# Order edges for the down steps, the scores and a convolution's weight split, and six gate/up pairs in the wide form, in a decoder layer of one core

## The chip, the cores and the metric

The kernel runs on one core of one Trainium2 chip. The metric is the device time of one launch in microseconds (us). The time of a kernel is the median of its runs; beside it stands one profiled execution, whose trace is what the tables and rows below come from. In the trace PE is TensorE's matmuls, PEld its weight loads, DVE VectorE, ACT ScalarE, POOL GpSimd and SP SyncE (which issues the weight transfers).

## The reference

One layer on `x` of 512 tokens by 1024 features, all in float32: a SwiGLU feed-forward, a merge of two token mixers (dilated attention and a gated linear recurrence), and a second feed-forward, with a norm before and after each.

```python
D_MODEL = 1024; SEQ = 512; N_ATTN_HEADS = 12; HEAD_DIM = 128; LRU_WIDTH = D_MODEL; CONV_WIDTH = 4; D_FF = 2816

def swiglu(x, w_gate, w_up, w_down):
    return (jax.nn.silu(x @ w_gate) * (x @ w_up)) @ w_down
...
    f = swiglu(rms_norm(h, ffn1_norm_pre[l]), ffn1_w_gate[l], ffn1_w_up[l], ffn1_w_down[l])
    h = h + 0.5 * rms_norm(f, ffn1_norm_post[l])
    u = rms_norm(h, mix_norm_pre[l])
    q, k, v, xr, yr, gl = jnp.split(u @ w_in[l], splits, axis=-1)
    ...  # attention in three groups of four heads (dilations 1, 4, 16), merged over the groups by their log-sum-exp
    attn_d = attn.astype(x.dtype).reshape(B, S, ATTN_OUT_WIDTH) @ w_attn_branch[l]
    rec = rg_lru_branch(xr, ...) * jax.nn.gelu(yr)       # convolution of width 4, two gates, a scan over the tokens
    rec_d = rec @ w_rec_branch[l]
    gates = jax.nn.sigmoid(gl).reshape(B, S, N_BRANCHES, D_MODEL)
    h = h + rms_norm((gates[:, :, 0] * attn_d + gates[:, :, 1] * rec_d) @ w_out[l], mix_norm_post[l])
    f = swiglu(rms_norm(h, ffn2_norm_pre[l]), ffn2_w_gate[l], ffn2_w_up[l], ffn2_w_down[l])
    return h + 0.5 * rms_norm(f, ffn2_norm_post[l])
```

## The kernel before

**Numbers.** Each float32 operand is split into a high part (its rounding to the fp32r type, written by an ACT copy, L302) and a low part (the rest, a DVE subtraction, L303). That pair of instructions is called a split. A product is then three matmuls into one PSUM tile: high by high, high by low, low by high (L729, L730, L731).

**Pairs.** Activations lie transposed, features on partitions and 512 tokens along the row. The 2816 hidden columns are 22 tiles, numbered f. For most f the gate tile and the up tile form a 2 by 2 block matrix (two halves of the inner dimension by gate and up), and the activations another (two halves of the inner dimension by two halves of the tokens, `HB` = 256). Their product is formed from seven products p1 to p7 in place of eight, each of four inner steps of 128 (`seventh`). The sums of weight blocks that this needs are made for each pair by `w_forms` on DVE (L691 to L696), followed by four splits called a, b, c, d: a is used by p1 and p2, b by p6 and p5, c by p7 and p4, d by p3. The raw weights of a pair are two transfers of 512 KB through SP into a ring of four `raw` tiles.

There are three ways to run a pair. `seven` keeps partial sums on DVE. `seven_on`, called narrow here, has its products in the order p1, p5, p6, p2, p7, p3, p4; it carries the sum on in PSUM: ACT copies a partial sum into the start of the next accumulator (L743), so that the following product adds to it. It is 84 matmuls of 256 columns. `seven_wide`, called wide here, takes the high and the low part of the activations in one matmul of 512 columns (L779) and the low weights by high activations in one of 256 (L780), with the two partial results in the two halves of a PSUM tile. It is 28 matmuls of each width; its partial sums are moved on as tiles of 512 columns (ACT, L784), and each result is folded from the two halves (ACT copy L790 and DVE addition L792; DVE L800 and the line after the branch in `sum_of`). It uses all five `acc` tiles of PSUM, `seven_on` four. The mixers' pairs (q and k, the two gates, the gated branch) are wide already. In the feed-forwards f = 0 to 5 (first) and 0 to 2 (second) are plain, f = 3 and 4 of the second are `seven`, and the rest are narrow.

**Down.** The down projection also runs by seven products, in four parts of four tiles f each (`SEVEN`, `STEPS_AT`), the last six tiles plainly. Each part has four steps i = 0 to 3; the step's weights are prepared by `d_forms` ("prepd") and used by `down7`, which issues 12 matmuls of 512 columns for each of its products (L1043 to L1045), 24 in most steps. The results are added up through `aux` tiles of PSUM: ACT copies a running sum into the tile before ("seeds", L1032) and out of it after (L1048). `ffn_order` writes out the order of the events: for each f the forms of the step, the forms of the next pair ("prep"), the pair ("prod"), the step.

**Order.** A scheduler fixes the order of the instructions on each engine when the kernel is built, by priorities. `tc.high_priority(offset=...)` raises what is inside: `AHEAD` = 100 for weight forms, `EVAC` = 200 for what empties PSUM. `tc.issue_after(ins)` keeps an instruction behind `ins` where both are on the same engine; it adds no semaphore. The order may therefore put a few matmuls of a down step, or of the scores of the attention (L1378 and L1379: first of head 0, ahead of a softmax), between two products of a pair. `state` is a dictionary in which the last split's instructions are kept under "split" (ACT) and "low" (DVE).

The convolution (`conv`) fetches the weights of each 128 columns with `fetch`, which splits them; the third group's first fetch stands beside the pair of the fourth gated branch, which is not wide.

Of the kernel before, what the change touches and what calls it, by code (L numbers as in the profile page):

```python
# [16 lines left out]
P = 128  # L17
# [3 lines left out]
NF = 22  # L21
FF_PARTS = ((0, 4), (4, 8), (8, 12), (12, 16), (16, 22))
NSTD = {1: 6, 2: 3}

SEVEN = range(4)
STEPS_AT = {1: ((6, 7, 7, 8), range(9, 13), range(13, 17), range(17, 21)),
# [4 lines left out]
HB = 256  # L31
# [152 lines left out]
def hybrid_layer(ctx: ExitStack, tc: tile.TileContext, xT: bass.AP, xN: bass.AP, wst: bass.AP,  # L184
# [537 lines left out]
    def seventh(t, w, p, ps, start):  # L722
        at = t[p].at
        if len(at(0, 0).shape) == 3:
            ps = ps.rearrange("q (b t) -> q b t", b=2)
        for k in range(4):
            ks = slice(k * P, (k + 1) * P)
            wh, wl, xh, xl = w[p][:, 0, ks], w[p][:, 1, ks], at(0, k), at(1, k)
            PE.matmul(ps, wh, xh, start=start and k == 0, stop=False, skip_group_check=True)  # L729
            PE.matmul(ps, wh, xl, start=False, stop=False, skip_group_check=True)  # L730
            PE.matmul(ps, wl, xh, start=False, stop=k == 3, skip_group_check=True)  # L731

    def seven_on(t, w, g0, g1, u0, u1):

        b, z, y, v = (acc_ps()[:, :HB] for _ in range(4))

        def copy(ps, dst=None):
            if dst is None:  # L740
                dst = tpool.tile([P, HB], F32, name="c", tag="c", bufs=CB)
            with tc.high_priority(offset=EVAC):
                ACT.activation(dst, ps, AF.Copy)  # L743
            return dst

        seventh(t, w, "p1", b, True)
        copy(b, y)
        seventh(t, w, "p5", z, True)
        c5 = copy(z)
        seventh(t, w, "p6", b, False)  # L750
        c6 = copy(b)
        seventh(t, w, "p2", y, False)
        g0(y)
        seventh(t, w, "p7", b, False)
        copy(b, v)
        u1(b, c5)
        seventh(t, w, "p3", z, False)
        g1(z, c6)
        seventh(t, w, "p4", v, False)
        u0(v)  # L760

    def seven_wide(t, w, g, u, seen=lambda ap: ap, then=lambda: None, sign=1.0):


        b, z, y, v, o = (acc_ps() for _ in range(5))

        def two(ps):
            return ps[:, :HB], ps[:, HB:]

        def product(p, ps, start):  # L770
            at = t[p].at
            part, cross = ps.rearrange("q (s c) -> q s c", s=2), two(ps)[1]
            if len(at(0, 0).shape) == 3:
                part = ps.rearrange("q (s b t) -> q s b t", s=2, b=2)
                cross = cross.rearrange("q (b t) -> q b t", b=2)
            for k in range(4):
                ks = slice(k * P, (k + 1) * P)
                wh, wl = w[p][:, 0, ks], w[p][:, 1, ks]
                PE.matmul(part, wh, at(BOTH, k), start=start and k == 0, stop=False, skip_group_check=True)  # L779
                PE.matmul(cross, wl, at(0, k), start=False, stop=k == 3, skip_group_check=True)  # L780

        def move(dst, src):
            with tc.high_priority(offset=EVAC):
                return ACT.activation(dst, src, AF.Copy).ins  # L784

        def fold(ps, dst=None, sign=1.0):
            out = tpool.tile([P, HB], F32, name="c", tag="c", bufs=CB) if dst is None else dst
            x, y_ = two(ps) if dst is None else map(seen, two(ps))
            with tc.high_priority(offset=EVAC):
                ACT.activation(out, x, AF.Copy, scale=sign)  # L790
                if sign > 0:
                    DVE.tensor_add(out, y_, out)  # L792
                else:
                    DVE.scalar_tensor_tensor(out, y_, sign, out, op0=ALU.mult, op1=ALU.add)
            return out

        def sum_of(dst, ps, c, sign=1.0):
            x, y_ = two(ps)
            with tc.high_priority(offset=EVAC):
                DVE.tensor_add(c, x, c)  # L800
                if sign > 0:
                    DVE.tensor_add(dst, seen(y_), seen(c))
                else:
                    DVE.scalar_tensor_tensor(dst, y_, sign, c, op0=ALU.mult, op1=ALU.subtract)

        product("p1", b, True)
        move(y, b)
        product("p5", z, True)
        c5 = fold(z)
        product("p6", y, False)  # L810
        move(v, y)
        c6 = fold(y)
# [46 lines left out]
    def ffn(n, x, r, forms_x, apool, pss):  # L859
# [82 lines left out]

        def prod(f, w):
            g, u = tmp("g"), tmp("u")
            if f >= FIRST_ON[n]:
                lo, hi = HALVES

                def g1(z, c6):
                    with tc.high_priority(offset=EVAC):
                        DVE.tensor_add(g[:, hi], z, c6)  # L950
                    ACT.activation(g[:, hi], g[:, hi], AF.Silu)

                def u1(b, c5):
                    with tc.high_priority(offset=EVAC):
                        DVE.tensor_add(u[:, hi], b, c5)

                def u0(v):
                    def put(dst, view):
                        for q, (h, src) in enumerate(zip(HALVES, (v, u[:, hi]))):
                            DVE.scalar_tensor_tensor(dst[:, q] if len(dst.shape) == 3 else dst[:, h], g[:, h], -1.0,  # L960
                                                     src, op0=ALU.mult, op1=ALU.mult)
                    into(f, put)

                seven_on(t, w, lambda y: ACT.activation(g[:, lo], y, AF.Silu), g1, u0, u1)
                return
            seven(t, w, acc_ps()[:, :HB], [g[:, h] for h in HALVES], [u[:, h] for h in HALVES])
            ACT.activation(g, g, AF.Silu)
            into(f, lambda dst, v: DVE.scalar_tensor_tensor(dst, v(g), -1.0, v(u), op0=ALU.mult, op1=ALU.mult))

# [64 lines left out]
        def down7(a, i, w):  # L1034
            x = sevens[a]
            gs = groups(i)
            for m, (p, k) in enumerate(gs):
                ps = seeded.pop((p, k))
                first = not follows(a, p)
                for j in range(2):  # L1040
                    xh, xl = (x[p][:, s_, j * HB + k * P:j * HB + k * P + P] for s_ in range(2))
                    wh, wl = (w[p][:, s_, j * T:(j + 1) * T] for s_ in range(2))
                    PE.matmul(ps, xh, wh, start=first and j == 0, stop=False, skip_group_check=True)  # L1043
                    PE.matmul(ps, xh, wl, start=False, stop=False, skip_group_check=True)  # L1044
                    PE.matmul(ps, xl, wh, start=False, stop=j == 1, skip_group_check=True)  # L1045
# [20 lines left out]

        keys = [(w, n, i) for i in range(NSTD[n]) for w in ("gate", "up")]
        forms = {}
        for ev in ffn_order(n):
            if ev[0] == "std":  # L1070
                j = ev[1]
# [6 lines left out]
                for step in steps[j:] if j == min(NSTD[n], 4) - 1 else steps[j:j + 1]:  # L1078
                    step()
            elif ev[0] == "prep":  # L1080
                forms[ev[1]] = w_forms(("gu", n, ev[1]))
            elif ev[0] == "prepd":
                forms[ev[1:]] = d_forms(*ev[1:])
            elif ev[0] == "seeds":
                for g in groups(ev[2])[:3]:
                    seed(ev[1], *g)
            elif ev[0] == "down7":
                down7(*ev[1:], forms.pop(ev[1:]))
            else:
                prod(ev[1], forms.pop(ev[1]))  # L1090
# [112 lines left out]
    with ExitStack() as mx:  # L1203
# [164 lines left out]
        def attend(hd, heads):  # L1368
# [6 lines left out]

            p0 = [facc[:, 0, :], facc[:, 1, :]]
            sp = [aux_ps(), aux_ps()]
            PE.matmul(sp[0][:, 0:128], q[0][:, 0:P], k[0][:, 0:P], start=True, stop=True)  # L1378
            PE.matmul(sp[0][:, 128:384], q[0][:, P:2 * P], k[0][:, 0:2 * P], start=True, stop=True)  # L1379
            for b in (2, 3):  # L1380
                PE.matmul(sp[1][:, (b - 2) * 256:(b - 1) * 256], q[0][:, b * P:(b + 1) * P],
# [127 lines left out]
    with ExitStack() as mx:  # L1509
# [44 lines left out]
        def conv(hd, then):  # L1554

            for c in (2 * hd, 2 * hd + 1):
                ps, w = acc_ps(), fetch(("in", 36 + c))
                if c % 2:
                    then()
                gemm(ps, w, um)  # L1560
# [300 lines left out]
```

## Time and profile before

| | us |
|---|---|
| median of 3 runs | 1209.59 |
| lowest to highest run | 1208.93 to 1209.86 |
| the profiled execution | 1209.61 |
| its span in the trace | 1207.8 |
| PE busy | 1198.6 (99%) |
| DVE busy | 1033.3 (86%) |
| ACT busy | 831.8 (69%) |
| weight transfers (512 KB), issue to landing | 3.5 |

The span is the stretch from the first to the last instruction in the trace; the execution is 1.81 longer than it. Busy time is the sum over an engine's instructions. The ends of matmuls are modelled, so neighbouring matmuls overlap in the rows: a matmul of 256 columns is shown as 0.28 long, and the next one starts 0.12 after it. Distances between starts are therefore what counts for PE. The mean granted clock of TensorE is 0.999 of full speed.

### The profile page before, as it was taken

The numbers are of one execution on the slowest core, as the hardware profiler recorded it, in microseconds if no ns is written. First come the engines' busy times: TensorE is split into PE (matmuls) and PEld (weight loads), VectorE is DVE, ScalarE is ACT, GpSimd is POOL, SyncE is SP. The second block draws the span as 40 slices with busy tenths as digits, with TensorE's granted clock in tenths as the row PEclk, the third lists the DMA queues.
The fourth block names the chain that finished last, engine by engine and source line by source line (L and its number), as shares of the span: only waits on it lengthen the run. The fifth ranks groups of instructions, "written<-read, shape, count | busy, mean of one in ns | idle before, by whom it ended". The sixth has DMA issues, their size and how long they took to land.

```text
span 1207.8 us, 18850 instructions
## 1 busy us (share of the span) xinstructions
PE 1198.6 (99%) x7222; PEld 1070.1 (89%) x7222; DVE 1033.3 (86%) x1626; ACT 831.8 (69%) x1447; POOL 26.1 (2%) x51
## 2 busy tenths in 40 slices
PE   9999999999999999999999999999999999999997
PEld 8889999999888888888888888888899999999996
DVE  7999888989689899999868999774799888889964
ACT  6566787887566576777736988734566687778763
POOL 0000000000011000000000000000100000000000
PEclk9999999999999999999999999999999999999999
DMA  7224343434725232222323532235443333333441
GB/s 267 88 92 139 120 139 109 137 117 150 250 106 154 71 101 91 89 87 80 122 67 110 176 121 88 88 107 189 140 142 121 121 125 117 128 120 126 125 173 70
DMA packets 45819, 149.77 MB, mean 124 GB/s; under 512 B 5152, under 2 KB 8608, under 8 KB 45728
## 3 DMA queue, kind: packets, MB, share of 16 engines
q1 hardware_dynamic: 38160, 131.09, 32.9%
q0 software_dynamic: 7280, 17.30, 4.3%
q8 instruction: 56, 0.92, 0.3%
q14 instruction: 35, 0.29, 0.1%
q10 hardware_dynamic: 288, 0.17, 0.0%
HBM read 138.06 MB, written 6.29 MB: 120 GB/s over the span
## 4 chain that ended last, share of the span: by engine, by line
PE 92%; DVE 4%; DMA 2%; ACT 1%; issue 1%; DVEq 0%; ACTq 0%
PE acc L779 10%; PE acc L729 9%; PE acc L731 9%; PE acc L730 9%; PE acc L315 7%; PE acc L317 7%; PE acc L316 7%; PE acc L780 5%; PE aux L1043 4%; PE aux L1044 4%; PE aux L1045 4%; PE acc L433 2%; PE acc L432 2%; PE acc L431 2%; DVE w L303 2%; DMA raw<-in_w 2%
## 5 line engine op out<-in xcount | busy, mean ns | idle before, releaser
L303 DVE TENSOR_TENSOR w<-raw,w 128x1024 fp32r<-128x1024 f32 (+1 forms) x272 | 296.9, 1097 | 32.2 <-ACT w L302 31.4
L302 ACT ACTIVATE w<-raw 128x1024 fp32r<-128x1024 f32 (+1 forms) x272 | 259.5, 958 | 90.0 <-PE acc L317 48.2
L729 PE MATMUL acc<-big,w 128*128 128x256 f32 x860 | 243.6, 283 | 0.0
L731 PE MATMUL acc<-big,w 128*128 128x256 f32 x860 | 243.4, 283 | 0.0
L730 PE MATMUL acc<-big,w 128*128 128x256 f32 x860 | 243.3, 283 | 0.0
L729 PEld LDWEIGHTS acc<-big,w 128*128 128x128 f32 x860 | 164.8, 192 | 1.8
L730 PEld LDWEIGHTS acc<-big,w 128*128 128x128 f32 x860 | 164.8, 192 | 1.5
L731 PEld LDWEIGHTS acc<-big,w 128*128 128x128 f32 x860 | 164.8, 192 | 0.0
L779 PE MATMUL acc<-big,w 128*128 128x512 f32 x380 | 136.5, 398 | 0.0
L780 PE MATMUL acc<-big,w 128*128 128x256 f32 x380 | 107.5, 283 | 0.0
L1043 PE MATMUL aux<-w,xf 128*128 128x512 f32 x224 | 87.3, 392 | 0.6 <-ACT w L302 0.6
L1044 PE MATMUL aux<-w,xf 128*128 128x512 f32 x224 | 87.5, 391 | 0.0
L1045 PE MATMUL aux<-w,xf 128*128 128x512 f32 x224 | 87.2, 389 | 0.0
L779 PEld LDWEIGHTS acc<-big,w 128*128 128x128 f32 x380 | 71.4, 188 | 16.0 <-ACT acc L784 0.2
L780 PEld LDWEIGHTS acc<-big,w 128*128 128x128 f32 x380 | 71.7, 189 | 0.3
L303 DVE TENSOR_TENSOR w<-s,w 128x1024 fp32r<-128x1024 f32 x51 | 62.2, 1220 | 3.2 <-ACT w L302 2.7
L315 PE MATMUL acc<-xf,w 128*128 128x512 f32 (+1 forms) x168 | 59.2, 354 | 0.0
L316 PE MATMUL acc<-xf,w 128*128 128x512 f32 (+1 forms) x168 | 58.7, 350 | 0.0
L317 PE MATMUL acc<-xf,w 128*128 128x512 f32 (+1 forms) x168 | 58.5, 349 | 0.0
L302 ACT ACTIVATE w<-s 128x1024 fp32r<-128x1024 f32 x51 | 53.9, 1057 | 6.2 <-PE acc L731 3.0
L779 PE MATMUL acc<-rb,w 128*128 128x512 f32 x152 | 55.5, 397 | 0.0
L743 ACT ACTIVATE c<-acc 128x256 f32<-128x256 f32 x68 | 25.8, 383 | 35.3 <-PE acc L731 35.3
(458 smaller groups left out, 2919.5 us busy)
## 6 DMA issues: line engine op xcount, KB each, us to landing
raw<-in_w SPq DMA_DIRECT2D x232, 512.0 KB, 3.5
big<-xf POOLq DMA_DIRECT2D x6, 512.0 KB, 3.3
gains<-in_rows POOLq DMA_DIRECT2D x5, 512.0 KB, 5.4
h<-in_x SPq DMA_DIRECT2D x8, 256.0 KB, 5.1
h<-in_xn POOLq DMA_DIRECT2D x4, 512.0 KB, 6.7
kept_m<-h POOLq DMA_DIRECT2D x4, 512.0 KB, 2.9
vals<-in_w SPq DMA_DIRECT2D x4, 512.0 KB, 6.0
h<-kept_m POOLq DMA_DIRECT2D x4, 512.0 KB, 6.2
```

What stands on the lines that cost most here:

```text
L302: state["split"] = ACT.activation(dh, src, AF.Copy).ins
L303: state["low"] = DVE.tensor_sub(dl, src, dh.bitcast(F32)).ins
L315: PE.matmul(ps, wh, xh, start=first, stop=False)
L316: PE.matmul(ps, wh, xl, start=False, stop=False)
L317: PE.matmul(ps, wl, xh, start=False, stop=last)
L729: PE.matmul(ps, wh, xh, start=start and k == 0, stop=False, skip_group_check=True)
L730: PE.matmul(ps, wh, xl, start=False, stop=False, skip_group_check=True)
L731: PE.matmul(ps, wl, xh, start=False, stop=k == 3, skip_group_check=True)
L779: PE.matmul(part, wh, at(BOTH, k), start=start and k == 0, stop=False, skip_group_check=True)
L780: PE.matmul(cross, wl, at(0, k), start=False, stop=k == 3, skip_group_check=True)
L1043: PE.matmul(ps, xh, wh, start=first and j == 0, stop=False, skip_group_check=True)
L1044: PE.matmul(ps, xh, wl, start=False, stop=False, skip_group_check=True)
```

## The change

It has four parts.

- Six pairs of the feed-forwards run as `seven_wide`: f = 10, 14, 18 in the first and 9, 13, 17 in the second, one in each cycle of four tiles, at the step i = 1 of a down part. Behind them stand one ACT silu and one DVE product of 512 columns in place of two of 256 each.
- Each matmul of `down7` is kept behind `state["product"]`, the last matmul of the last product written before it (p4 of the pair in front). In the same way the first scores' matmul of each head is kept behind the last product written before it.
- The weight forms of the next pair are kept behind the splits of the down step's weights ("prepd"), on ACT and on DVE.
- The fetch of the convolution's column block 4 is kept behind `state["kept"]`, the ACT copy of b into v of the last narrow pair (that of the fourth gated branch).

```diff
+WIDE = {1: (10, 14, 18), 2: (9, 13, 17)}
...
-            PE.matmul(ps, wl, xh, start=False, stop=k == 3, skip_group_check=True)
+            state["product"] = PE.matmul(ps, wl, xh, start=False, stop=k == 3, skip_group_check=True).ins
...
-                ACT.activation(dst, ps, AF.Copy)
+                state["copied"] = ACT.activation(dst, ps, AF.Copy).ins
...
         copy(b, v)
+        state["kept"] = state["copied"]
...
+                last = PE.matmul(cross, wl, at(0, k), start=False, stop=k == 3, skip_group_check=True)
+            state["product"] = last.ins
...
-            if f >= FIRST_ON[n]:
+            if f in WIDE[n]:
+                seven_wide(t, w, *([x[:, h] for h in HALVES] for x in (g, u)))
+            elif f >= FIRST_ON[n]:
...
+                    with tc.issue_after(state["product"]):
+                        PE.matmul(ps, xh, wh, start=first and j == 0, stop=False, skip_group_check=True)
+                        PE.matmul(ps, xh, wl, start=False, stop=False, skip_group_check=True)
+                        PE.matmul(ps, xl, wh, start=False, stop=j == 1, skip_group_check=True)
...
+        behind = []
...
-                forms[ev[1]] = w_forms(("gu", n, ev[1]))
+                with ExitStack() as edges:
+                    while behind:
+                        edges.enter_context(tc.issue_after(behind.pop()))
+                    forms[ev[1]] = w_forms(("gu", n, ev[1]))
             elif ev[0] == "prepd":
                 forms[ev[1:]] = d_forms(*ev[1:])
+                if True:
+                    behind[:] = [state["split"], state["low"]]
...
-            PE.matmul(sp[0][:, 0:128], q[0][:, 0:P], k[0][:, 0:P], start=True, stop=True)
+            with tc.issue_after(state["product"]):
+                PE.matmul(sp[0][:, 0:128], q[0][:, 0:P], k[0][:, 0:P], start=True, stop=True)
...
-                ps, w = acc_ps(), fetch(("in", 36 + c))
+                ps = acc_ps()
+                with tc.issue_after(state.pop("kept")) if hd == 2 and c == 4 else nullcontext():
+                    w = fetch(("in", 36 + c))
```

More of the change, by code (lines that the diff above doesn't have):

```diff
@@ L779, in product @@
                 PE.matmul(part, wh, at(BOTH, k), start=start and k == 0, stop=False, skip_group_check=True)
-                PE.matmul(cross, wl, at(0, k), start=False, stop=k == 3, skip_group_check=True)
+                last = PE.matmul(cross, wl, at(0, k), start=False, stop=k == 3, skip_group_check=True)
+            state["product"] = last.ins
         def move(dst, src):
@@ L965, in prod @@
                 return
-            seven(t, w, acc_ps()[:, :HB], [g[:, h] for h in HALVES], [u[:, h] for h in HALVES])
+            else:
+                seven(t, w, acc_ps()[:, :HB], [g[:, h] for h in HALVES], [u[:, h] for h in HALVES])
             ACT.activation(g, g, AF.Silu)
@@ L1042, in down7 @@
                     wh, wl = (w[p][:, s_, j * T:(j + 1) * T] for s_ in range(2))
-                    PE.matmul(ps, xh, wh, start=first and j == 0, stop=False, skip_group_check=True)
-                    PE.matmul(ps, xh, wl, start=False, stop=False, skip_group_check=True)
-                    PE.matmul(ps, xl, wh, start=False, stop=j == 1, skip_group_check=True)
+                    with tc.issue_after(state["product"]):
+                        PE.matmul(ps, xh, wh, start=first and j == 0, stop=False, skip_group_check=True)
+                        PE.matmul(ps, xh, wl, start=False, stop=False, skip_group_check=True)
+                        PE.matmul(ps, xl, wh, start=False, stop=j == 1, skip_group_check=True)
                 dst, sign = sum_at(p)
```

## The prediction

> **What bounds the kernel now.** I read the page first, then the waits of TensorE, then windows and timelines around each edit. Times are us. Section 1 and the engine line of section 4 (the chain that ended last):
>
> ```profile
> span 1207.8 us, 18850 instructions
> PE 1198.6 (99%) x7222; PEld 1070.1 (89%) x7222; DVE 1033.3 (86%) x1626; ACT 831.8 (69%) x1447; POOL 26.1 (2%) x51
> PE 92%; DVE 4%; DMA 2%; ACT 1%; issue 1%; DVEq 0%; ACTq 0%
> raw<-in_w SPq DMA_DIRECT2D x232, 512.0 KB, 3.5
> ```
>
> The reader sees that PE works nearly all the span and carries 92% of the chain. So only two things can shorten it: fewer or cheaper PE issues, and the few places where PE stands. DVE at 86% is the next bound; ACT and DMA have room. The last line (512 KB of weights, issue to landing) is needed further down. The waits of PE, the rows that answer to the edits (us in all, times, longest):
>
> ```profile
> PE aux L1378 <- DVE qk L792: 0.7, 1, 0.7
> PE aux L1043 <- ACT w L302: 0.6, 3, 0.2
> PE acc L729 <- ACT acc L743: 0.4, 1, 0.4
> ```
>
> These are exactly a scores' matmul, three down matmuls and a product waiting for a copy. A row counts only idle time behind the modelled end of the matmul before, so the real loss is larger; I take it from starts.
>
> The profiled run took 1209.61: the span of 1207.8 and 1.81 outside it. The median of the three runs is 1209.59, 0.02 away, so what is taken off the profiled run is taken off the median. 0.2% is 2.4: faster means under 1207.2, slower over 1212.0.
>
> **Part 1, six pairs in the wide form.** Windows: start:end, length, then busy time and instructions of PE, PEld, DVE, ACT, POOL, then granted clock, DMA share and GB/s. First a narrow pair, then two wide pairs of the gated branch that the kernel already has, then two cycles of four pairs with their down steps, one of each feed-forward.
>
> ```profile
> 181.05:191.12 10.07, 10.07 (x85) 10.07 (x84) 9.20 (x14) 7.88 (x15) 0.00 (x0) 1.00 0.32 106
> 623.18:642.78 19.60, 19.60 (x114) 17.06 (x112) 15.26 (x27) 15.43 (x24) 0.00 (x0) 1.00 0.28 88
> 224.95:284.39 59.44, 59.44 (x421) 56.07 (x420) 53.71 (x69) 47.53 (x82) 0.00 (x0) 1.00 0.36 121
> 1012.59:1072.68 60.09, 59.88 (x422) 56.19 (x421) 50.97 (x69) 46.66 (x81) 0.00 (x0) 1.00 0.37 122
> ```
>
> A narrow pair is 84 matmuls of 256 columns in 10.07, 0.120 each. A wide pair is 28 of 512 and 28 of 256 columns: 19.60 / 2 = 9.80. Six pairs save 6 x 0.27 = 1.6. The granted clock is 1.00 in all rows, so no clock differs between the forms.
>
> The Trainium skill has a rule that speaks against this size ("TensorE: Matmul & The Clock Gate", section "Wait — 56ns, not 53.3ns?"): warm back-to-back matmuls start N columns over 2.4 GHz plus about 2.5 ns apart, so joining two matmuls spares only the fixed part. As an estimate from that page, 28 fewer matmuls would save 28 x 2.5 ns = 0.07 a pair, 0.4 in all; the trace's 0.120 for 256 columns is more than that rule gives, so here the trace disagrees and decides.
>
> What the wide form adds lies on DVE and ACT. Groups by line (busy, mean ns, idle before and what ended it); the three of `seven_on` and the 128x512 one are from the window 165.51 to 224.95:
>
> ```profile
> L792 DVE TENSOR_TENSOR c<-acc,c 128x256 f32<-128x256 f32 x38 | 15.8, 419 | 5.3 <-ACT c L790 5.0
> L800 DVE TENSOR_TENSOR c<-acc,c 128x256 f32<-128x256 f32 x38 | 14.9, 416 | 0.6
> L955 DVE TENSOR_TENSOR u<-acc,c 128x256 f32<-128x256 f32 x4 | 1.7, 417 | 0.0
> L950 DVE TENSOR_TENSOR g<-acc,c 128x256 f32<-128x256 f32 x4 | 1.7, 416 | 0.0
> L960 DVE SCALAR_TENSOR_TENSOR tt<-g,acc 128x256 f32<-128x256 f32 x4 | 1.7, 414 | 0.0
> L925 DVE SCALAR_TENSOR_TENSOR tt<-tt 128x512 f32<-128x512 f32 x1 | 0.7, 684 | 0.0
> L784 ACT ACTIVATE acc<-acc 128x512 f32<-128x512 f32 x57 | 33.5, 588 | 14.2 <-PE acc L780 11.3 <-DVE e L1443 1.1 <-DVE xch L1421 1.1
> ```
>
> Narrow, DVE: u1, g1 and two products, 0.417 + 0.416 + 2 x 0.414 = 1.66. Wide: four folds (L792), two sums of two steps (L800), one product of 512 columns: 4 x 0.419 + 4 x 0.416 + 0.684 = 4.02. That is 2.36 more a pair. ACT has three moves of 0.588 (1.76) more; its four copies of 256 columns stay. The busiest cycle goes from 53.71 to 56.07 of DVE in about 59.2, 95%, the other quoted one to 53.3 in 59.8, 89%. DVE is therefore still not the bound of a cycle. On average the cost is nothing, hidden by 3.1 of free DVE time a cycle; the order of steps has to be looked at.
>
> That order I followed by hand behind a wide pair of the first feed-forward, whose last fold stands ahead of the next pair's weight forms on DVE. Let E be the end of its last product. The rows for the steps and, in the present order, how the same chain ends on ACT and what it is for on PE:
>
> ```profile
> L303 DVE TENSOR_TENSOR w<-raw,w 128x1024 fp32r<-128x1024 f32 x13 | 15.9, 1221 | 1.9 <-ACT w L302 1.9
> L692 DVE TENSOR_TENSOR s<-s,raw 128x512 f32<-128x512 f32 x4 | 2.8, 689 | 1.7 <-DMA raw<-in_w 1.7
> 216.92 1.05 ACT L302 ACTIVATE w<-raw 128x1024 fp32r<-128x1024 f32 x1
> 219.52 0.37 ACT L743 ACTIVATE acc<-acc 128x256 f32<-128x256 f32 x1
> 220.76 0.28 PE L729 MATMUL acc<-big,w 128*128 128x256 f32 x1
> ```
>
> Fold about 0.6, four weight sums of 0.69, a stt of 0.684 and two splits of 1.22 end at about E + 6.4. PE first does a down step of 24 matmuls at 0.228 (5.5) and p1 (1.44), and wants the b forms at E + 6.9: 0.5 left. The c split ends 1.22 later, E + 7.6, and lets the next gate weights start; they land 3.5 later, E + 11.1. Then on ACT come the a and b splits, a silu half and the copy of b into v. In the rows this stretch lasts from 216.92 to 219.89, 2.97; it would end near E + 14.1. PE wants that copy before p4, at E + 5.5 + 6 x 1.44 = E + 14.1 (in the rows the copy has 0.9 in hand). So this copy is due about when it is wanted. Between nothing (the splits run closer than in those rows) and 0.6 (landing a little late), three times; I take 0.1 to 0.15 each, near the lower end, since the sum closes to 0.0. Behind wide pairs of the second feed-forward the same sum leaves over 1.5, and it costs nothing.
>
> **Part 2, down behind the pair's product.** PE's timeline (start, length): a stand in the second feed-forward and, for the pace, an undisturbed down step; then pieces of the chain: the split in front of the stand, and the two other stands.
>
> ```profile
> 941.02 0.28 PE L731 MATMUL acc<-big,w 128*128 128x256 f32 x1
> 941.51 0.72 PE L1043 MATMUL aux<-w,xf 128*128 128x512 f32 x2 [0.21 <-ACT w L302]
> 942.07 0.28 PE L729 MATMUL acc<-big,w 128*128 128x256 f32 x1
> 147.22 0.40 PE L1043 MATMUL aux<-w,xf 128*128 128x512 f32 x1
> 147.46 0.40 PE L1044 MATMUL aux<-w,xf 128*128 128x512 f32 x1
> 940.51 0.95 ACT w L302
> 1014.39 0.73 PE aux L1043 x2
> 1074.48 0.73 PE aux L1043 x2
> ```
>
> Two down matmuls stand between p1 and p5 and want a split that ACT ends at 941.46. PE could have gone on at 941.14: 0.37 lost. The two then take 0.56 in place of 2 x 0.23, 0.10 more. So 0.47, three times by the waits (941.5, 1014.4, 1074.5): 1.4. Behind the pair's last product the split is over 8 old. What is late next? The copies of down's sums, and through them the seeds of the following groups; down steps already run so in most cycles, without a row in the waits. Nothing taken for it. The weight forms that the change puts behind a down split on ACT and DVE wait for what stood beside them: at most 0.3 at the first such pair (f6, product p7, behind two 128x1024 splits), taken as 0.1.
>
> **Part 3, scores behind a product.**
>
> ```profile
> 418.52 0.28 PE L780 MATMUL acc<-big,w 128*128 128x256 f32 x1
> 419.46 0.49 PE L1378 MATMUL aux<-qk 128*128 128x128 f32 x2 [0.66 <-DVE qk L792]
> 429.64 0.59 PE L1379 MATMUL aux<-qk 128*128 128x256 f32 x2
> 429.89 0.58 PE L779 MATMUL acc<-big,w 128*128 128x512 f32 x1
> 430.30 0.28 PE L780 MATMUL acc<-big,w 128*128 128x256 f32 x1
> ```
>
> The first scores could start at 418.64 and wait for the fold that writes q and k until 419.46: 0.82. The later pair of scores breaks a product: 429.89 to 430.30 is 0.41 where 0.23 is usual, 0.18. Behind the third pair's last product q and k are long folded. The softmax of head 0 starts later by about a pair; it has the next pairs to hide in. One break stays, 0.1. Gain 0.9; bounds 0.6 (the softmax pushes back 0.3) and 1.0.
>
> **Part 4, a convolution's weight split behind the copy.**
>
> ```profile
> 688.56 0.28 PE L731 MATMUL acc<-big,w 128*128 128x256 f32 x1
> 689.22 0.39 PE L729 MATMUL acc<-rb,w 128*128 128x256 f32 x1 [0.38 <-ACT acc L743]
> 687.84 1.05 ACT L302 ACTIVATE w<-raw 128x1024 fp32r<-128x1024 f32 x1
> 688.79 0.37 ACT L743 ACTIVATE acc<-acc 128x256 f32<-128x256 f32 x1
> ```
>
> p4 starts 0.54 late (688.68 to 689.22) because the copy stands behind a split of 1.05. With the copy ahead it ends about 688.7 and p4 stands for 0.1 at most: gain 0.43 (0.3 to 0.54). The split comes 0.4 later; its weights are next on PE after the rest of this pair, some microseconds on.
>
> **Sum.** 1.6 + 1.4 + 0.9 + 0.4 = 4.3, less 3 x 0.13 + 0.1 = 0.5: 3.8 to 3.9. 1209.6 - 3.9 = **1205.7**. Own range: all bounds good, 1.6 + 1.4 + 1.0 + 0.54 = 4.5, 1205.0; all bounds bad, 1.6 + 1.4 + 0.6 + 0.3 - 3 x 0.6 - 0.3 = 1.8, 1207.8.
>
> **The rivals.**
> - A: the joining of matmuls spares little among down steps, because the 0.27 was measured in an undisturbed stretch. Its bounds are 0 and 0.27 a pair; at the lower quarter, 0.07, 1.2 are missing: 1206.9. Against: both rows are dense. The skill's 2.5 ns, above, would come to the same place.
> - B: the copy behind wide pairs stalls at its upper bound, 3 x 0.6 = 1.8 where 0.4 is in the sum: 1207.1 to 1207.8. For: the sum closes to 0.0.
> - C: the edges only shift the stands to another product or down group (gain 0 from parts 2 to 4): 1209.6 - 1.6 + 0.5 = 1208.5. Against: every freed instruction is one whose data come early, by microseconds.
> - D, slower: DVE becomes the bound around the wide pairs. From the point where its lag behind E passes the 0.5 in hand at the b forms, each further microsecond stands on PE. If all of the 2.36 less 0.5 does so six times, 6 x 1.86 = 11.2 against 4.3: 1216.5. Against: 3.1 free a cycle, and the second feed-forward's larger room.
> - E: the build's order leaves something unmoved. The instruction order of the changed kernel shows six wide pairs and each moved step, so it is left at nearly nothing.
>
> **How the numbers follow.** Forecast 0.60, A 0.12, B 0.11, C 0.08, D 0.08, E 0.01. Faster: forecast 0.58, A 0.11, half of B 0.06, C 0.01: 0.76. Slower: D and a little more, 0.09. Within: 0.15. The range takes the forecast's good end with something for stands not counted (1204.0) and reaches past B and C's middle (1208.6); D and half of C stay out.
>
> **What would show it.** After: PE's waits without the L1378, L1043 and L729 rows above; six windows of about 9.80 in place of 10.07; about 7222 - 168 = 7054 matmuls; DVE busy up by 6 x 2.36 = 14 and ACT by about 10. Wrong would be: new waits of PE for DVE's splits (w L303) or for the copy into v right behind the wide pairs (B, D), wide windows above 10 (A, D), or waits of the same size at other products (C).

## The result, and the profile after

The changed kernel takes 1213.38 us (median of 8 runs, 1212.5 to 1214.18), the kernel before 1209.72 in the same runs: ratio 1.0029, 95% interval 1.002 to 1.0038. It is slower by 3.7 us; forecast was a gain of 3.9, to 1205.7, with a range of 1204.0 to 1208.6. The profiled execution took 1213.6, its span is 1211.8. Lines of the page after:

```profile
span 1211.8 us, 18611 instructions
PE 1200.5 (99%) x7054; PEld 1061.2 (88%) x7054; DVE 1044.6 (86%) x1656; ACT 840.0 (69%) x1459; POOL 26.1 (2%) x51
PE 86%; DVE 5%; ACT 5%; DMA 2%; issue 1%; DVEq 0%; ACTq 0%
raw<-in_w SPq DMA_DIRECT2D x232, 512.0 KB, 3.7
```

PE issues 168 matmuls fewer, as it should, and the span is 4.0 longer. DVE is busy for 11.3 more and ACT for 8.2 more, where 14 and about 10 were forecast. In the chain that ended last, ACT has gone from 1% to 5% and PE from 92% to 86%. The waits of PE after:

```profile
PE acc L730 <- ACT acc L744: 1.3, 2, 0.9
PE acc L730 <- ACT c L744: 1.2, 2, 0.6
PE aux L1418 <- DVE facc L1399: 0.3, 1, 0.3
PE acc L732 <- DVE w L304: 0.2, 1, 0.2
PE acc L781 <- DVE qk L805: 0.2, 1, 0.2
```

(Lines moved: L744 is L743 of before, L730 to L732 are L729 to L731, L304 is L303; L1418 is a later group of the scores.) The three rows that the edges were aimed at are gone, but for a rest at the convolution. New ones stand in their place: two waits for the copy of b into v (`acc`), two for the copy that p7 waits for (`c`). Where they lie is read from windows by stage (start:end, length, busy time and instructions of PE, PEld, DVE, ACT, POOL). The stages are the first feed-forward from its first pair, the attention from its first q and k pair, the pair beside the convolution, and the second feed-forward. First before, then after, then three pairs after: f = 11, f = 12 and the wide f = 14.

```profile
72.26:310.00 237.74, 237.74 (x1681) 224.29 (x1680) 210.27 (x277) 182.50 (x309) 3.28 (x6) 1.00 0.41 133
407.36:601.19 193.83, 193.17 (x1189) 171.05 (x1188) 181.86 (x403) 137.91 (x305) 0.00 (x0) 1.00 0.30 96
680.00:690.74 10.74, 10.36 (x86) 10.14 (x84) 10.74 (x17) 9.98 (x16) 2.16 (x4) 1.00 0.61 213
898.55:1168.69 270.14, 269.52 (x1934) 255.04 (x1933) 235.56 (x314) 200.28 (x340) 2.66 (x5) 1.00 0.40 130
```

```profile
72.10:314.12 242.02, 239.31 (x1598) 220.18 (x1597) 216.16 (x293) 186.15 (x315) 3.28 (x6) 1.00 0.40 129
411.33:605.35 194.02, 193.48 (x1189) 170.85 (x1188) 181.56 (x403) 138.25 (x305) 0.00 (x0) 1.00 0.31 96
684.06:694.38 10.32, 10.32 (x86) 10.13 (x84) 10.32 (x17) 9.56 (x16) 2.16 (x4) 1.00 0.61 208
902.28:1172.66 270.38, 269.93 (x1850) 250.70 (x1849) 241.37 (x329) 203.91 (x346) 2.66 (x5) 1.00 0.39 129
152.52:163.92 11.40, 10.53 (x86) 10.19 (x85) 10.01 (x13) 8.35 (x16) 0.00 (x0) 1.00 0.42 139
166.66:177.78 11.12, 10.51 (x85) 10.16 (x84) 9.92 (x15) 7.84 (x15) 0.00 (x0) 1.00 0.46 143
198.79:208.67 9.88, 9.88 (x57) 8.56 (x56) 5.89 (x9) 7.33 (x14) 0.00 (x0) 1.00 0.53 154
```

Stage by stage: first feed-forward +4.28, attention +0.19, convolution -0.42, second feed-forward +0.24; the other stretches add -0.3. So nearly all the loss is in the first feed-forward, where the two pairs behind f = 10 and the two behind f = 14 take 11.1 to 11.4 in place of 10.07, 4.5 together. Behind f = 18 there is no such loss. A wide pair takes 9.88: it saves 0.19, not 0.27.

The chain behind f = 10, whose last product ends at E = 147.06 (the start of the matmul behind it). Pieces of the chain that ended last (start, length, what), then rows of the timeline of DVE, ACT and PE:

```profile
153.03 2.35 DVE w L304 x2
155.37 0.02 issue
155.39 4.30 DMA raw<-in_w
```

```profile
148.53 0.41 DVE L795 TENSOR_TENSOR u<-acc,u 128x256 f32<-128x256 f32 x1
148.87 0.68 DVE L692 TENSOR_TENSOR s<-raw 128x512 f32<-128x512 f32 x1
...
159.78 1.06 ACT L303 ACTIVATE w<-raw 128x1024 fp32r<-128x1024 f32 x1 [1.46 <-DMA raw<-in_w]
161.95 0.38 ACT L744 ACTIVATE acc<-acc 128x256 f32<-128x256 f32 x1
...
161.23 0.28 PE L732 MATMUL acc<-big,w 128*128 128x256 f32 x1
162.38 0.38 PE L730 MATMUL acc<-big,w 128*128 128x256 f32 x1 [0.87 <-ACT acc L744]
```

The wide pair's last fold (L795) stands on DVE ahead of all forms of f = 11 (L692 on). The c split of f = 11 ends at E + 8.3; only then does the next transfer start; it lands at E + 12.6; ACT's splits follow, and behind them in ACT's queue the copy that p4 of f = 11 wants at 161.35. p4 starts at 162.38, 1.03 late. At f = 15 p4 is 0.57 late in the same way, and p5 has waited 0.37 before that for the low half of a split on DVE.

The second stall, at p7 of f = 12, goes back to the same landing. Pieces of its chain:

```profile
159.79 0.10 DVE s L693
171.26 0.70 DVE tt L929
171.98 0.03 ACT xf L303
172.95 0.37 ACT c L744
173.37 0.39 PE acc L730
```

From 159.79 to 171.95 DVE stands idle for less than 0.1 in all. It has the forms of f = 12, a sum of the down step and, as the last piece, a quarter sum of the down part (L929) to do. The split of that quarter is on ACT ahead of the copy that p7 wants, and p7 starts 0.77 late.

### The profile page after: what moved, and what is told of

Its sections match the earlier page's. It is cut to its first block, busy times and chain, and to the rows that moved or that the text cites. A ratio compares the mean times of both kernels' runs of the same rounds, so it can differ in the third digit from the quotient of the medians.

```text
span 1211.8 us, 18611 instructions
## 1 busy us (share of the span) xinstructions
PE 1200.5 (99%) x7054; PEld 1061.2 (88%) x7054; DVE 1044.6 (86%) x1656; ACT 840.0 (69%) x1459; POOL 26.1 (2%) x51
## 4 chain that ended last, share of the span: by engine, by line
PE 86%; DVE 5%; ACT 5%; DMA 2%; issue 1%; DVEq 0%; ACTq 0%
PE acc L781 12%; PE acc L316 7%; PE acc L318 7%; PE acc L317 7%; PE acc L730 7%; PE acc L732 7%; PE acc L731 7%; PE acc L782 6%; PE aux L1050 3%; PE aux L1051 3%; PE aux L1052 3%; DVE w L304 2%; DMA raw<-in_w 2%; ACT w L303 2%; PE acc L432 2%; PE acc L434 2%
## 5 line engine op out<-in xcount | busy, mean ns | idle before, releaser
L304 DVE TENSOR_TENSOR w<-raw,w 128x1024 fp32r<-128x1024 f32 (+1 forms) x272 | 295.5, 1097 | 32.3 <-ACT w L303 30.9
L303 ACT ACTIVATE w<-raw 128x1024 fp32r<-128x1024 f32 (+1 forms) x272 | 259.2, 959 | 78.5 <-PE acc L318 47.1
L730 PE MATMUL acc<-big,w 128*128 128x256 f32 x716 | 203.7, 285 | 2.9 <-ACT acc L744 1.3
L732 PE MATMUL acc<-big,w 128*128 128x256 f32 x716 | 202.7, 283 | 0.2 <-DVE w L304 0.2
L731 PE MATMUL acc<-big,w 128*128 128x256 f32 x716 | 202.6, 283 | 0.0
L781 PE MATMUL acc<-big,w 128*128 128x512 f32 x524 | 187.0, 397 | 0.2 <-DVE qk L805 0.2
L782 PE MATMUL acc<-big,w 128*128 128x256 f32 x524 | 147.4, 281 | 0.0
L730 PEld LDWEIGHTS acc<-big,w 128*128 128x128 f32 x716 | 137.0, 191 | 6.3 <-ACT acc L744 2.6
L731 PEld LDWEIGHTS acc<-big,w 128*128 128x128 f32 x716 | 137.2, 192 | 1.1
L732 PEld LDWEIGHTS acc<-big,w 128*128 128x128 f32 x716 | 137.1, 192 | 0.6 <-DVE w L304 0.4
L781 PEld LDWEIGHTS acc<-big,w 128*128 128x128 f32 x524 | 98.4, 188 | 22.8 <-PE acc L782 0.4
L782 PEld LDWEIGHTS acc<-big,w 128*128 128x128 f32 x524 | 98.8, 189 | 0.4
L304 DVE TENSOR_TENSOR w<-s,w 128x1024 fp32r<-128x1024 f32 x51 | 62.1, 1218 | 0.8 <-ACT w L303 0.6
L303 ACT ACTIVATE w<-s 128x1024 fp32r<-128x1024 f32 x51 | 53.9, 1057 | 7.9 <-PE acc L732 4.2
L787 ACT ACTIVATE acc<-acc 128x512 f32<-128x512 f32 x75 | 44.3, 591 | 15.6 <-PE acc L782 12.7
```

Of the source, the lines that this page charges most:

```text
L303: state["split"] = ACT.activation(dh, src, AF.Copy).ins
L304: state["low"] = DVE.tensor_sub(dl, src, dh.bitcast(F32)).ins
L732: state["product"] = PE.matmul(ps, wl, xh, start=False, stop=k == 3, skip_group_check=True).ins
L782: last = PE.matmul(cross, wl, at(0, k), start=False, stop=k == 3, skip_group_check=True)
```

## The experiments

"Stage" below is a stage's length as in the windows above. Each run is compared with the kernel before in its own runs; ratios have 95% intervals.

**Without wide pairs** (`WIDE = {1: (), 2: ()}`), all edges kept. 

> The changed kernel with no wide pair, all edges kept. Theory T (the wide pairs f = 10 and 14 delay the next pair's weight forms on DVE, so its transfer, so the copy of b into v): the stalls of 4.55 us behind f = 10 and 14 and of 0.7 behind f = 9 and 13 of the second feed-forward go, and with them the 6 x 0.19 that wide pairs save: 1213.4 - 4.1 = 1209.3 us. Rival R (it is the edge that puts the next pair's forms behind the down split that makes them late, with or without wide pairs): most of the 4.55 stays, about 1213 us.

Measured: 1208.71, ratio 0.9996 (0.9987 to 1.0004); first feed-forward 237.94, second 269.90. R fell: without wide pairs the stalls behind f = 10 and 14 are gone. The four edges together are worth about nothing, and without wide pairs they cost the first feed-forward 0.2.

**Wide pairs only**, no edges. 

> The kernel before with the six wide pairs and none of the edges. T: it has the stalls of the changed kernel behind f = 10 and 14 (4.55) less 1.15 for the wide form: about 1213 us. R: no such stall, 1209.7 - 1.15 = 1208.6 us.

Measured: 1211.03, 1.0016 (1.0007 to 1.0025); first feed-forward 240.17, second 269.87. Between the two forecasts: the wide pairs alone cost the first feed-forward 2.4, the wide pairs with the edges 4.3. The stands are at another place, though. Both p4 and p7 are in time; in f = 12 and 16 two down matmuls stand between p1 and p5 and wait for a split on ACT, 1.65 and 0.84 late:

```profile
167.71 0.72 PE L1050 MATMUL aux<-w,xf 128*128 128x512 f32 x2 [1.49 <-ACT w L303]
```

The next run has the down edge as well, and there the stands are at p7 of the same pairs.

**The edge on the forms taken away**, the rest of the change kept.

```diff
-                if True:
+                if False:
                     behind[:] = [state["split"], state["low"]]
```

> The changed kernel without the edge that keeps the next pair's weight forms behind the down split. T: the stalls behind f = 10 and 14 stay; only the 0.32 at f = 6 and the 0.58 at each p7 behind f = 6, 10, 14 of the second feed-forward shrink: about 1212 us. R: all goes, 1213.4 - 4.55 = 1208.9 us.

Measured: 1209.91, 1.0004 (0.9995 to 1.0013). Both stages fell:

```profile
71.86:312.25 240.39, 238.46 (x1598) 219.96 (x1596) 215.99 (x292) 185.50 (x315) 3.29 (x6) 1.00 0.39 132
900.39:1169.31 268.92, 268.64 (x1850) 250.38 (x1849) 240.48 (x329) 203.76 (x346) 2.66 (x5) 1.00 0.39 130
```

Against the changed kernel that is -1.6 and -1.5: this one edge costs 3.1 of the change. The stall of f = 11 is gone (10.07; the transfer that its p4 depends on lands at E + 10.0), that of f = 12 is not (0.88 late at its p7). The total lies between the two forecasts, nearer to R's 1208.9.

**Wide only at f = 18 in the first feed-forward** (`WIDE = {1: (18,), 2: (9, 13, 17)}`), all edges. 

> The changed kernel with f = 18 as the only wide pair of the first feed-forward (the second keeps its three). In the trace f = 18 has no stall behind it. T: 1213.4 - 4.55 + 0.38 = 1209.2 us. R: about 1213 us.

Measured: 1208.81, 0.9997 (0.9988 to 1.0006); first feed-forward 238.30. As theory T said, f = 10 and 14 carry the loss; a smaller stand (0.46, for a copy) is left behind f = 18.

**The down edge alone.** 

> The kernel before with the down edge alone. Theory T (the three stands of 0.47 in the second feed-forward go and nothing takes their place, as in the kernel with wide pairs and no edge on the forms, whose second feed-forward took 268.9 in place of 270.1): second feed-forward 268.7, 1209.4 - 1.4 = 1208.0 us. Rival R (the freed time comes back at p7, as in the kernels with all edges, where the copy that p7 waits for is 0.23 late three times): second feed-forward about 269.9, 1209.2 us.

Measured: 1208.0, 0.9989 (0.998 to 0.9998); second feed-forward 269.24. The three stands are gone, and a new one came. It is at p6, the third product of a pair, which adds to the tile b and waits until ACT has copied b into y:

```profile
1074.92 0.39 PE L730 MATMUL acc<-tx,w 128*128 128x256 f32 x1 [0.24 <-ACT acc L744]
```

It starts 0.40 late. Of 1.4 there remain 0.9. With the edge on the forms beside it (the run without wide pairs) the stage is 269.90: that edge takes 0.66 of it back.

**Down and convolution edges, wide pairs in the second feed-forward only.** 

> Down edge, convolution edge and the three wide pairs of the second feed-forward; no wide pair in the first, no edge on the scores or on the forms. The stages measured one by one add up to: first feed-forward as before, scores as before, convolution -0.42, second feed-forward -1.2: 1209.4 - 1.6 = 1207.8 us. If the parts depend on each other (a rival to reading the stages as independent), it stays within 0.5 of 1209.4.

Measured: 1207.2, 0.9981 (0.9972 to 0.999): the fastest of all.

```profile
73.01:310.74 237.73, 237.73 (x1681) 224.29 (x1680) 210.32 (x277) 183.75 (x309) 3.29 (x6) 1.00 0.40 133
898.89:1167.34 268.45, 268.45 (x1851) 250.33 (x1850) 240.38 (x329) 203.78 (x346) 2.67 (x5) 1.00 0.39 131
```

PE is busy through the whole of both stages. The 1207.8 was added up from stages of other kernels, so the stages can be read as nearly independent.

**Wide pairs without the fold additions**, all edges. 

> The changed kernel, whose six wide pairs in the feed-forwards leave out the four DVE additions that fold the two halves of an accumulator (4 x 0.42 = 1.7 us of DVE a pair, so the result lacks the cross terms). T (the next pair's forms are late because DVE is busy with the wide pair's folds): the c split behind f = 10 ends 1.5 to 1.7 earlier, the 4.55 of stalls behind f = 10 and 14 falls to under 1.5: about 1210 us. Rival R (ACT's three moves, or the fifth accumulator, make it late): stalls stay, about 1213 us.

Measured: 1212.82, 1.003 (1.0019 to 1.0042); first feed-forward 239.96, second 271.09. In the first, the c split of f = 11 ended at E + 7.6 in place of 8.3, the transfer landed at E + 11.3, and p4 was in time. Smaller stands came at p6 of f = 11 and 15 (0.45 and 0.58, for the copy into y), and p7 of f = 12 and 16 was 0.38 and 0.24 late. The four pairs behind f = 10 and 14 together lose 2.0 in place of 4.5, not under 1.5 as T had it. But the build put the later instructions of DVE and ACT in another order, and the second feed-forward got three new waits of 0.2 to 0.7. The total therefore tells nothing; the first stage supports T in part.

**The scores edge alone.** 

> The kernel before with the scores edge alone. T (the stand of 0.8 goes, and others of 0.2 to 0.5 take its place behind it): the stretch from the first q and k pair to the recurrence's first product takes 193.8 to 194.1, as in all kernels with this edge; total 1209.4 to 1209.7 us. Rival R (those others come from the wide pairs' or the down edge's shift of the streams ahead): 192.9, total 1208.5 us.

Measured: 1210.21, 1.0004 (0.9995 to 1.0013); attention 194.12 against 193.83. The stand of 0.8 is gone, and PE stands elsewhere, in its timeline and in its waits:

```profile
440.93 1.16 PE L1418 MATMUL aux<-qk 128*128 128x128 f32 x8
518.37 0.38 PE L1418 MATMUL aux<-qk 128*128 128x128 f32 x1 [0.30 <-DVE facc L1399]
```

```profile
PE aux L1418 <- DVE facc L1399: 0.3, 1, 0.3
PE aux L1438 <- DVE xch L1435: 0.2, 1, 0.2
```

The later groups of the scores (L1418) now follow the first at once. The first scores take two `aux` tiles, the next group the third, and the group at 440.93 needs a fourth where there are three: it waits until DVE has read the first scores out (L1399). T holds for the place of the stands. That the stage is longer than before is not shown: over all kernels of this document it took 193.64 to 194.14 with this edge on every head and 193.61 to 193.93 without it.

**Wide pairs at other places**, without the edges on scores and forms: `1: (12, 16, 20)`. 

> Down and convolution edges, the second feed-forward's three wide pairs, and in the first feed-forward wide pairs at f = 12, 16, 20, the last step of a down part, in place of 10, 14, 18 (no edges on scores or forms). T (what decides is how much DVE work and how many PE microseconds stand behind the wide pair: f = 10 is followed by a pair with a short down step of 12 matmuls, f = 12 by three full steps): the first feed-forward takes 237.7 - 3 x 0.19 = 237.2 to 238, total 1206.7 to 1207.5. Rival R (any wide pair of the first feed-forward makes the next forms late): 239 to 240, total 1209 us.

Measured: 1208.47, 0.999 (0.9981 to 0.9999); first feed-forward 237.43. No stall: the place decides, as T said. What gives room at these places was not looked into, and the total is above T's 1207.5 and above that of the version without wide pairs in the first feed-forward.

The same with `1: (9, 13, 17)`. 

> As the run before with f = 9, 13, 17 in the first feed-forward, the first step of a down part. T: one pair more than f = 10 lies between the wide pair and the short step, so the lag can be worked off in part: 237.3 to 238.5 for the first feed-forward, total 1206.8 to 1208. R: 239 to 240, total 1209 us.

Measured: 1210.14, 1.0002 (0.9993 to 1.001); first feed-forward 240.91, longer than either forecast. The longest stand is at p6 of f = 16, 1.51 late, which waits for the copy of b into y:

```profile
230.21 0.39 PE L730 MATMUL acc<-tx,w 128*128 128x256 f32 x1 [1.35 <-ACT acc L744]
```

The distance to the short down step, on which T's forecast for this place rested, is not what decides.

**As much DVE work in narrow pairs**, no wide pair, all edges: at f = 10 and 14, two operations like this behind c5, behind c6 and behind the last product.

```diff
+                with tc.high_priority(offset=EVAC):
+                    for _ in range(2):
+                        DVE.scalar_tensor_tensor(c, x, 0.0, c, op0=ALU.mult, op1=ALU.add)
```

> The changed kernel with no wide pair, and in the narrow pairs f = 10 and 14 of the first feed-forward six DVE operations of 128x256 that leave the result as it is (two after each of the copies c5 and c6, two that read the last accumulator; about 2.5 us a pair, as much as a wide pair adds). T (DVE time in front of the next forms is enough to make the stall): the first feed-forward takes 237.9 + 2 to 4 = 240 to 242, total 1211 to 1213 us. Rival R (it takes the wide form's ACT moves or its fifth accumulator): 237.9, total 1208.7 us.

Measured: 1208.92, 0.9995 (0.9986 to 1.0004).

```profile
72.17:310.11 237.94, 237.94 (x1681) 224.36 (x1680) 213.63 (x290) 183.21 (x309) 3.28 (x6) 1.00 0.40 132
```

DVE is 3.9 busier than without them (209.71) and the stage is 237.94 as before. DVE time alone makes no stall. In this kernel the forms of f = 11 begin before the pair ends (L692 at 144.28, E at 147.33). R's time came, but its causes (ACT's moves, the fifth accumulator) are not shown by that: the run without fold additions keeps both, and p4 is in time there.

**The scores edge for head 0 only**, on top of the fastest version. 

> Down and convolution edges, the second feed-forward's wide pairs, and the scores edge for head 0 alone. If the stands that the scores edge brings are those of the later heads (0.46 and 0.38 in the trace with the edge alone), the stretch of the attention takes 193.8 - 0.8 + 0.2 = 193.2, total 1206.6 us. If the stand of head 0 comes back at the next group of its scores and further on (the three aux tiles are then full), 193.7, total 1207.2 us.

Measured: 1207.84, 0.9986 (0.9978 to 0.9995); attention 193.56 against 193.77 without it. The waits at L1418 came back as in the second forecast. A gain of 0.2 can't be told from the spread of that stage.

**The third down step's sum behind the next forms**, the rest of the change kept: in the first feed-forward `d_forms` of i = 2 stands under `issue_after` of the last split. 

> The changed kernel with one more edge: in the first feed-forward the third down step's operations (the sum L1001 and its split) are kept behind the next pair's weight forms, not ahead of them. Theory T2 (not DVE's time but the order on DVE makes the stall: in the changed kernel the sum, waiting 1.6 us for its transfer, and the wide pair's last fold stand ahead of all forms of f = 11 and 15): the c split behind f = 10 ends about 1.4 earlier, the copy into v is in time, the first feed-forward takes 242.0 - 2 to 4 = 238 to 240, total 1209.5 to 1211.5 us. Rival R2 (the wide pair's DVE work alone makes it late, wherever the forms stand): 242, total 1213 us.

Measured: 1212.96, 1.0029 (1.0018 to 1.0039); first feed-forward 243.53, worse. The last split of f = 11 did end earlier, at E + 6.6. But the moved sum also sets a tile of the ring of raw weights free later. A transfer that had started at 145.85 in the changed kernel now comes at 152.99, and three started between 152.99 and 154.72; the one that is wanted, now the second, took 6.2 and landed at E + 12.8, p4 1.29 late. A piece of its chain, and the first weight sum of f = 12 that uses the transfer:

```profile
153.59 6.18 DMA raw<-in_w
```

```profile
159.86 0.69 DVE L693 TENSOR_TENSOR s<-s,raw 128x512 f32<-128x512 f32 x1 [1.81 <-DMA raw<-in_w]
```

Behind f = 10 T2 fell: the order of the DVE steps moved, the landing didn't. Behind f = 14 the landing did move, from E + 12.5 to E + 11.6 (E is the end of f = 14 here); there p4 was 0.17 late and the pair f = 15 took 10.33 in place of 11.21. The stage is longer all the same, for f = 20 takes 11.71: it waits for the low half of a split.

```profile
214.44:224.77 10.33, 10.32 (x86) 10.12 (x84) 9.32 (x13) 7.23 (x14) 0.00 (x0) 1.00 0.59 203
291.24 0.39 PE L732 MATMUL acc<-big,w 128*128 128x256 f32 x1 [1.07 <-DVE w L304]
```

So the order on DVE matters, and this edge pays for it elsewhere.

**The forms of f = 11 and 15 late, with narrow pairs**: `w_forms` called after `prod` and kept behind its last DVE product. 

> The changed kernel with no wide pair, and the weight forms of f = 11 and 15 put behind the last DVE product of the narrow pairs f = 10 and 14, the place that they have in the changed kernel behind the wide pairs. T2: the c split ends about 7.5 behind the pair's last product (8.3 in the changed kernel), and the stalls of p4 and of the next pair's p7 come without any wide pair: the first feed-forward takes 239.5 to 241.5 in place of 237.9, total 1210.5 to 1212.5 us. R2: narrow pairs have the time to spare, 238, total 1208.8 us.

Measured: 1209.03, 1.0 (0.9991 to 1.0008); first feed-forward 237.93, no stall. The transfer started at E + 6.5 and landed at E + 10.1. So the late place alone doesn't do it either: T2's stalls did not come.

Put side by side, the landing of that transfer behind E decides p4: 10.0 (wide, no edge on the forms), 10.1 (late forms, narrow) and 11.3 (no fold additions) are in time, 11.6 (sum moved, f = 15) is 0.17 late, 12.6 (changed kernel) 1.03, 12.8 (sum moved, f = 11) 1.29. The point is near 12.63 - 1.03 = 11.6. In these runs it took the wide pair's DVE work with the forms behind it, or a slow landing, to pass it. Both together in narrow pairs were not run.

**The second stall**, p7 of f = 12 and 16. Its chain in the run without the edge on the forms (pieces of the chain of waits):

```profile
169.17 0.65 DVE s L693
169.81 0.61 DVE tt L929
170.45 0.03 ACT xf L303
171.41 0.38 ACT c L744
```

A weight sum of f = 13 (L693; its row shows no wait) stands on DVE ahead of the last quarter sum of the down part (L929); the quarter's split stands on ACT behind that, and the copy that p7 wants behind the split. In the changed kernel itself no sum of f = 13 stands ahead of L929; there DVE's queue is late as a whole, as shown above. The run puts the forms of f = 13 and 17 behind that quarter sum:

```diff
+                    if n == 1 and ev[1] in (13, 17):
+                        edges.enter_context(tc.issue_after(state["quarter"]))
```

> The changed kernel without the edge on the forms (the run e3_no_behind, whose first feed-forward took 240.4), and with the weight forms of f = 13 and 17 kept on DVE behind the part's last quarter sum (L929 in the trace), not ahead of it. T3 (the second stall, of 0.9 at p7 of f = 12 and 0.8 of f = 16, is a matter of queues: weight sums of the pair after next, which wait for their transfer, stand on DVE ahead of that quarter sum, the split of the quarter stands on ACT behind it, and the copy that p7 waits for behind the split): both stalls go, the first feed-forward takes 237.9 to 238.8, total 1207.5 to 1208.5 us. Rival (DVE is short of time there with wide pairs, in whatever order): 240, total 1209.9 us.

Measured: 1208.79, 0.9993 (0.9984 to 1.0002).

```profile
71.68:310.94 239.26, 238.64 (x1598) 219.94 (x1596) 215.03 (x292) 184.69 (x315) 3.28 (x6) 1.00 0.39 132
```

The pairs f = 12 and 16 fell from 11.35 and 10.94 to 10.28 and 10.35, the stage by 1.1. T3 holds for these two in the kernel without the edge on the forms; stage and total missed T3's 238.8 and 1208.5, and the rival's times fit no better. The rest over 238 lies for the most part behind f = 18 (0.7 in the pair f = 20 and 0.7 in its down step), which was not looked into further.

## Why the prediction was wrong, point by point

By stage the forecast was about -0.3 for the first feed-forward, -0.9 for the attention, -0.4 for the pair beside the convolution and -2.2 for the second feed-forward. Against +4.28, +0.19, -0.42 and +0.24 the misses are 4.6, 1.1, 0 and 2.4.

- **What bounds the kernel**: right. PE is 99% busy, and the only matters are what PE issues and where it stands.
- **Wide form, 0.27 a pair**: right in kind, too large. The row it came from is two wide pairs end to end; among down steps it is 9.88, 0.19 a pair, 1.1 in all for 1.6. The estimate from the Trainium skill ("TensorE: Matmul & The Clock Gate", section "Wait — 56ns, not 53.3ns?") was 0.07; the measured 0.19 lies between, nearer to the rows.
- **The chain behind a wide pair of the first feed-forward, 0.1 to 0.15 each**: this step failed. The chain was the right one, from the fold to the copy into v, and due at about the time it was wanted. But the c split ended at E + 8.3 for the 7.6 that was summed, and the landing took 4.3 for the median 3.5. What was mis-sized in the first part is the fold: it was done at E + 1.8, not at about E + 0.6, because a down sum (L1001) had waited 1.6 for its transfer and a down split stood behind it, both ahead of the wide pair's sums; the steps behind the fold ran 0.6 quicker than summed (6.5 for 7.1). With a slack of 0.0, the two errors of 0.7 and 0.8 made p4 1.03 late. And the sum ended at the first pair: the stall of the pair after it, nearly as large, was in no bound. 4.5 measured (with the edge of the next item), 0.4 in the sum, 1.8 at its worst. Behind the wide pairs of the second feed-forward, put at nothing, copies stood for 1.0 in the changed kernel and for 0.1 in the fastest one; how much of this the wide pairs cause by themselves was not separated.
- **The edge that keeps the forms behind a down split, 0.1**: this step failed as well, with 3.1 of the miss of 7.6. It was costed at the first pair f = 6 alone (0.2 there). With the wide pairs it costs 1.6 in the first feed-forward and 1.5 in the second, where it makes the copy for p7 0.23 late and the next one 0.14 at each cycle; without wide pairs 0.2 and 0.7. It is what put the forms of f = 11 behind the fold. Without it p4 is in time, and the wide pairs still lengthen the first feed-forward by 2.6, mostly at p7 of f = 12 and 16 and behind f = 18.
- **Down edge, 1.4**: mechanism right, 0.9 remained alone; the copy into y at one p6 took most of the rest.
- **Scores edge, 0.9**: failed. What is late next was said to be the softmax, hidden by the next pairs; it is the next scores, for want of a free `aux` tile, and the edge holds for all four heads where only head 0 had a stand. The gain is about nothing in place of 0.9.
- **Convolution edge, 0.43**: right, 0.42 to 0.48 in every run that had it.
- **The rivals**: B was the mechanism of the first stall. Its price of 1.8 is about what p4 lost at f = 11 and 15, 1.03 and 0.57 and about 0.1 behind each, but by luck: it had three places of 0.6 and there were two; the second stall and the edge were not in it. C, that an edge only shifts the stands, is what the scores' edge did. A was right in part: 0.19 a pair, within its bounds of 0 and 0.27. D (DVE as the bound of a cycle) is not it, as the run with more DVE work showed, though the total came out slower, as D alone had it. But two signs of D came in small: p5 of f = 11 and 15 waited 0.1 and 0.4 for a split on DVE, and behind the late landing DVE ran for 12 us without a gap ahead of p7. DVE's free 3.1 a cycle is real, and no help: part of it went in waiting for transfers (1.6 ahead of L1001, 1.1 ahead of L693) with the work queued behind.

## What to carry to other kernels

Where a chain is worked out by hand to a slack of about nothing, the forecast is not "a tenth" but the spread of its terms, and it has to be followed into the pairs behind it. An edge that orders one queue is to be costed at every place where it holds, not where it was wanted: here one of four edges cost 3.1 us, and without it and the scores' edge, and with the wide pairs in the second feed-forward only, a loss of 0.29% became a gain of 0.19%. Ask of each removed wait which buffers the freed instruction takes earlier: the scores' edge gained nothing, since the next group wanted a fourth tile where there were three.

## What the runs showed of the hardware

A 512 KB weight transfer has a median landing of 3.5 in the kernel before; in the changed kernel the one that mattered took 4.30, as the first of three started within 2.1 us, and where three started within 1.7 us the second took 6.18. Why three in such a burst were this slow in one kernel and took 3.6 to 4.2 in another (late forms, started within 2.4) was not tried. After a wait, the first two matmul starts of a narrow product are 0.22 apart in place of 0.12 (in the changed kernel 162.38 and 162.60; the row at 162.38 is 0.38 long, not 0.28), so each stand costs about 0.1 more than its wait.
